# A decoder layer on one NeuronCore: two of four weight sums of the branch and gate products made in the SBUF ring by accumulating loads, and the products put in another order

## Chip, core and metric

The kernel runs on one core of one Trainium2 chip, from one launch. The metric is the time of the core for one execution in microseconds (us), as the median of several runs. Five engines with an instruction stream each work side by side: PE (TensorE, matrix products), ACT (ScalarE), DVE (VectorE), POOL (GpSimd) and SP (SyncE). Here SP issues the DMAs that load weights, and POOL issues those that copy and add in DRAM. Each engine executes its own stream in order; semaphores tie the streams together.

## What is computed

One layer: an input projection gives queries, keys and values for three token mixers and three gates; each mixer's output is projected (a branch), multiplied by the sigmoid of its gate and summed; then an output projection, LayerNorm, a squared-ReLU MLP and a gated input embedding. All in float32.

```python
proj = x @ w_in
(da_q, da_k, da_v, sb_q, sb_k, sb_v, dl_q, dl_k, dl_v, gates) = jnp.split(proj, ...)
g = jax.nn.sigmoid(gates).reshape(B, S, N_BRANCHES, D)
merged = (g[:, :, 0] * (o_da @ w_branch_da) + g[:, :, 1] * (o_sb @ w_branch_sb)
          + g[:, :, 2] * (o_dl @ w_branch_dil))
m = merged @ w_out
x = layer_norm(DEEPNORM_ALPHA * x + m, ln1_g, ln1_b)
c = jnp.square(jax.nn.relu(x @ w_up)) @ w_down
ple = jax.nn.sigmoid(x @ w_ple_gate) * (p @ w_ple)
x = layer_norm(DEEPNORM_ALPHA * x + c + ple, ln2_g, ln2_b)
```

S is 512, D is 1024. The branch weights of `w_branch_dil` (branch i=2) and `w_branch_da` (branch i=0) are 512x1024, `w_ple_gate` is 1024x1024.

## The kernel before

**Splits.** A float32 product is made of three fast ones: every operand is split into a high and a low part (`h`, `lo`), and PE computes h·h, h·lo and lo·h into one PSUM bank. For a weight chunk of 128x1024, `split_next` (L229) issues the cast of the raw chunk on ACT (L243, `wh<-raw`) and the subtract on DVE (L245, `wl<-raw,wh`). Raw chunks lie in a ring of RAW = 6 slots, which SP fills in order as slots come free (`fill`, L194, the load at L213); the split parts lie in rings of RING = 6.

**Seven products.** Large products are done with seven block products in place of eight (p = 1 to 7, Strassen's scheme in Winograd's form). The weight is cut into quarters w[0] to w[3]. Products 1, 2 and 4 use the quarters 0, 1 and 3 as they are; 5, 6, 7 and 3 use sums of two to four quarters. Those sums are made in DRAM on POOL's queue well ahead: `sum_steps` (L1083) yields one copy or one accumulating DMA (`accum_op` add) at a time, from `up_steps` (eight steps for all four sums) or `two_steps` (four steps for the sums of 5 and 6), and `issue` (L1116) ties each to the main stream. How fast they are yielded is set by a credit that each work item adds to: its size times its `rate` (default set at L825).

**Sums in the ring.** There is a second way, `chained` (L180), used by the value pair and by the gate products: the operand of product 7 is the one of product 1 plus a quarter, the operand of 3 that of 6 plus a quarter. `then_add` (L171) puts the quarter onto the raw slot by an accumulating DMA on POOL's queue as soon as the slot's first split is issued, and the slot is then split again:

```python
def add():
    nc.gpsimd.dma_start(s["raw"], src, accum_op=OP.add, max_dma_last_dim=4096)
c["then"] = add
return chunk_of(s)
```

**The places of the change.** `seven` (L603) with `gate_chain` (L668) makes the gate columns of one mixer: seven products in the order 1, 2, 7, 6, 4, 5, 3, two chunks to a product, two row halves r. Products 1, 6, 5 and 3 of a half share one PSUM bank ("x"), 7 and 4 another ("y"); `done` evacuates them into the tiles `graw`: by an ACT copy (L695), or a DVE add that also adds an earlier tile (L688 for product 4, L691 for product 5). Product 3 starts in bank x when product 5 of the same half has been evacuated from it.

`branch_seven` (L759) follows each gate chain: the branch of mixer i = 2, then of i = 0. It has one chunk to a product (K is 256 for a block), so its chunks follow each other twice as fast as those of a gate. Its forms of the mixer's output (`o7`, `o6`, `o4`, split at L271 and L272) come from `branch_forms` (L727). `pleg_items` (L991) is the gate of the input embedding: seven products of two chunks, beside LayerNorm 1, in which POOL computes the small tile `lr` (L872). Items follow each other in a list; the splits for the next items are issued ahead of their matmuls as ring slots allow, so that the first chunks of a branch are split while PE still works on the gate chain.

Of the kernel before, what the change touches and what calls it, by code (L numbers as in the profile page):

```python
# [10 lines left out]
F32 = mybir.dt.float32  # L11
# [7 lines left out]
P = 128  # L19
# [36 lines left out]
def trunk(tc, a, out):  # L56
    nc = tc.nc
    es = ExitStack()
    with es:
# [108 lines left out]
        def chunk(src, w):  # L168
            return chunk_of(load(src, w))
# [96 lines left out]
        def item(cs, mm, ev, need=None, bank=None, size=1.0):  # L266
            items.append({"c": cs, "mm": mm, "ev": ev, "need": need, "bank": bank, "size": size})
# [451 lines left out]
                         bank=at_bank if tt == 1 and not half else None)  # L719
                    items[-1]["rate"] = 2.4  # L720

        bsum = {i: [dram.tile([P, 1024], F32, name=f"bsum{i}_{j}") for j in range(4)] for i in (0, 2)}
        of = {}
        LATE = {0: 0, 2: 4}

        def branch_forms(i):

            o = [oT.pop(4 * i + k) for k in range(4)]
            f = {p: slot(f"o{p}") for p in (7, 6, 4)}

            def parts(p):
                return [f[p][:, c] for c in (HB, HC)]

            def whole(p):
                h, lo = split(f.pop(p), f"o{p}")
                of[p] = [(h[:, c], lo[:, c]) for c in (HB, HC)]

            for k in range(2):
                nc.vector.tensor_sub(parts(7)[k], o[2 + k][:, HC], o[k][:, HC])
            yield  # L740
            for p, q, k0 in ((6, 7, 0), (4, 6, 2)):
                for k in range(2):
                    nc.vector.scalar_tensor_tensor(parts(p)[k], parts(q)[k], -1.0, o[k0 + k][:, HB],
                                                   op0=OP.mult, op1=OP.subtract)
                yield
            sp = {k: split(o[k], "oT") for k in (2, 3)}
            yield
            for k in range(2):
                nc.vector.tensor_sub(o[k][:, HC], o[k][:, HB], o[k][:, HC])
                sp[k] = split(o[k], "oT")  # L750
            for p, k0, c in ((1, 0, HB), (5, 0, HC), (2, 2, HB), (3, 2, HC)):
                of[p] = [[t[:, c] for t in sp[k0 + k]] for k in range(2)]
            yield
            for p, n in ((7, LATE[i]), (6, LATE[i] // 4), (4, 0)):
                whole(p)
                for _ in range(n + 1):
                    yield

        def branch_seven(i, behind):  # L759

            s, b, cs = {}, {}, {}
            for p in (2, 1, 7, 6, 4, 5, 3):
                for r in range(2):
                    if not r:
                        blk = {1: 0, 2: 1, 4: 3}.get(p)
                        cs[p] = chunk(bsum[i][{5: 0, 6: 1, 7: 2, 3: 3}[p]] if blk is None else
                                      a["wbq"][i // 2, blk].rearrange("p k n -> p (k n)"), 1024)

                    def bank(p=p, r=r):
                        name = {1: "x", 6: "x", 5: "x", 3: "x", 7: "y", 4: "y", 2: "z"}[p]  # L770
                        if p in (1, 2, 7):
                            b[name, r] = at_bank()
                        return b[name, r]

                    def mm(ps, p=p, r=r):
                        q, c = slice(r * P, r * P + P), cs[p]
                        for k in range(2):
                            n = slice(k * 512, k * 512 + 512)
                            h, lo = of[p][k]
                            go, end = k == 0 and p in (1, 2, 7), k == 1 and p in (2, 3, 4)  # L780
                            nc.tensor.matmul(ps, h[:, q], c["h"][:, n], start=go, stop=False, skip_group_check=True)
                            nc.tensor.matmul(ps, h[:, q], c["l"][:, n], start=False, stop=False, skip_group_check=True)
                            nc.tensor.matmul(ps, lo[:, q], c["h"][:, n], start=False, stop=end, skip_group_check=True)

                    def ev(ps, p=p, r=r):
                        if p in (2, 7, 6):
                            s[p, r] = slot("b0")
                            nc.scalar.copy(s[p, r], ps)
                            return
                        v, to = {1: (2, (r, 0)), 4: (6, (r, 1)), 5: (7, (2 + r, 1)), 3: (None, (2 + r, 0))}[p]  # L790
                        if v is not None:
                            nc.vector.tensor_add(s[v, r], s[v, r], ps)
                        g = sg.pop((i, *to))
                        nc.vector.tensor_mul(g, g, ps if v is None else s[v, r])
                        m = merged[to]
                        (nc.vector.tensor_add if p in (1, 3) else nc.vector.tensor_sub)(m, m, g)
                    item([cs[p]] if r else [], mm, ev, need=[cs[p]], bank=bank, size=0.25)
                    items[-1]["rate"] = 1.0
                    to = {2: (r, 0), 7: (r, 1), 6: (2 + r, 1), 4: (2 + r, 0)}.get(p)
                    if to:  # L800
                        def pre(to=to):
                            sg[(i, *to)] = gate_sig(i, *to)
                        items[-1]["pre"] = pre
                    for t in behind.get((p, r), ()):
                        turn_item(*t)
# [16 lines left out]

        last_plain = len(items)
        for j, it in enumerate(items):
            it.setdefault("rate", 2.8 if j < 25 else 0.0 if j < 31 else 2.6)  # L825
        def first_gate(tt, half):
            g = gate_sig(1, tt, half)
            nc.vector.tensor_mul(merged[tt, half], merged[tt, half], g)
# [162 lines left out]
        def pleg_items():  # L991
# [5 lines left out]
            def gate(r, to, g, sign, z=None):  # L997
                tt, half = r + 2 * to[1], to[0]
                nc.scalar.activation(g, g if z is None else z, AF.Sigmoid, scale=sign)
                gated[tt, half] = g  # L1000
# [11 lines left out]
                    for _ in range(2):  # L1012
                        yield

            def operand(p, kp):
                blk = {1: 0, 2: 1, 4: 3}.get(p)
                src = a["wg"][kp, blk] if blk is not None else None
                return chunk(gsum[kp][{5: 0, 6: 1, 7: 2, 3: 3}[p]] if src is None else
                             src.rearrange("p k n -> p (k n)"), 1024)

            cs = {}
            for p in (2, 1, 7, 6, 4, 5, 3):
                for r in range(2):
                    name = {1: "x", 6: "x", 5: "x", 3: "x", 7: "y", 4: "y", 2: "z"}[p]
                    if not r:
                        cs[p] = [operand(p, kp) for kp in range(2)]

                    def bank(p=p, r=r, name=name):
                        if p in (1, 2, 7):
# [12 lines left out]
                            nc.tensor.matmul(ps, lo[:, q], c["h"][:, n], start=False, stop=end, skip_group_check=True)  # L1042

                    def ev(ps, p=p, r=r):
                        if p in (2, 7, 6):
                            s[p, r] = slot("sg2")
                            nc.scalar.copy(s[p, r], ps)
                        if p == 1:
                            nc.vector.tensor_add(s[2, r], s[2, r], ps)
                            gate(r, (0, 0), s[2, r], 1.0)  # L1050
# [1165 lines left out]
```

## Time and profile before

| | |
|---|---|
| median of three runs | 1036.57 us (1036.25 to 1037.67) |
| the profiled execution | 1035.76 us |
| its span, first to last instruction | 1033.6 us |
| mean granted clock of PE | 0.998 |
| ACT casts of weight chunks, L243 | 257, mean 1049 ns |
| DVE subtracts of weight chunks, L245 | 257, mean 1222 ns |
| DMA traffic | 249.19 MB, mean 241 GB/s |
| DMAs that POOL issues: share of 16 engines | 44.6% |
| DMAs that SP issues: share of 16 engines | 35.4% |

A row of the profile's tables by line has the line, the engine, the operation, and the tiles as out<-in, with buffer numbers left out. Rows in order of time begin with start and duration in us from the span's start; "x2" joins two of a kind that followed each other, and the bracket at the end gives the idle time of the engine before the row and what ended it. A DMA row on POOL is the issue alone; the time to landing is listed apart. Matmul rows overlap, since PE is pipelined: their starts tell the pace.

### The profile page before, as it was taken

What the parts mean: (1) busy time and instruction counts of PE and PEld (TensorE: products, weight loads), DVE (VectorE), ACT (ScalarE), POOL (GpSimd) and SP (SyncE); (2) the same over time, 40 slices, a digit from 0 to 9 for tenths busy, and PEclk for the clock granted to TensorE, in tenths of its full rate; (3) what the DMA queues carried; (4) which work ended last, traced back from release to release, by engine and by line L of the source; (5) the groups of instructions that cost most, each with busy time, mean ns of one, the idle gap of its engine ahead of it and who ended that gap; (6) DMA issues with size and microseconds to landing.
All of it is one profiled execution on the core that took longest, in us unless ns stands there. A gap on an engine that the chain in (4) does not pass through costs nothing.

```text
span 1033.6 us, 15019 instructions
## 1 busy us (share of the span) xinstructions
PE 1025.3 (99%) x5434; PEld 880.5 (85%) x5434; DVE 782.9 (76%) x1412; ACT 593.0 (57%) x1012; POOL 180.6 (17%) x271
## 2 busy tenths in 40 slices
PE   9999999999999999999999999999999999999997
PEld 7888888889888888888888888889999899899886
DVE  7888667758764657779788895798768777777966
ACT  7565544535434646576575743776666556566651
POOL 0002411121211232411011030111111111111001
PEclk9999999999999999999999999999999999999999
DMA  8349969495976999977889895479999999999512
GB/s 310 122 159 272 287 184 226 107 295 146 282 187 212 272 276 289 252 203 202 249 250 223 269 320 201 142 215 339 333 311 336 301 303 331 306 298 308 185 61 81
DMA packets 71321, 249.19 MB, mean 241 GB/s; under 512 B 8808, under 2 KB 9592, under 8 KB 71248
## 3 DMA queue, kind: packets, MB, share of 16 engines
q0 software_dynamic: 32464, 116.21, 44.6%
q1 hardware_dynamic: 38208, 131.13, 35.4%
q8 instruction: 42, 0.69, 0.3%
q10 hardware_dynamic: 576, 0.92, 0.2%
q14 instruction: 31, 0.25, 0.1%
HBM read 246.10 MB, written 98.59 MB: 333 GB/s over the span
## 4 chain that ended last, share of the span: by engine, by line
PE 97%; DVE 2%; ACT 0%; issue 0%; DVEq 0%
PE mm L87 10%; PE mm L89 10%; PE mm L88 10%; PE at L1300 4%; PE at L1301 4%; PE at L1302 4%; PE at L618 3%; PE at L620 3%; PE at L619 3%; PE mm L495 2%; PE mm L497 2%; PE mm L496 2%; PE at L89 1%; PE at L88 1%; PE at L87 1%; PE at L910 1%
## 5 line engine op out<-in xcount | busy, mean ns | idle before, releaser
L243 ACT CAST wh<-raw 128x1024 fp32r<-128x1024 f32 x257 | 268.5, 1049 | 237.0 <-PE mm L88 127.1
L245 DVE TENSOR_TENSOR wl<-raw,wh 128x1024 fp32r<-128x1024 f32 x257 | 312.2, 1222 | 118.9 <-ACT wh L243 117.6
L87 PE MATMUL mm<-xhT,wh 128*128 128x512 f32 x302 | 119.2, 395 | 0.0
L89 PE MATMUL mm<-xhT,wl 128*128 128x512 f32 x302 | 118.3, 392 | 0.0
L88 PE MATMUL mm<-xlT,wh 128*128 128x512 f32 x302 | 118.2, 392 | 0.0
L1300 PE MATMUL at<-wh,hh 128*128 128x512 f32 x188 | 73.7, 392 | 0.0
L1301 PE MATMUL at<-wl,hh 128*128 128x512 f32 x188 | 73.7, 392 | 0.0
L1302 PE MATMUL at<-wh,hl 128*128 128x512 f32 x188 | 73.1, 389 | 0.0
L87 PE MATMUL mm<-x1hT,wh 128*128 128x256 f32 x256 | 72.8, 285 | 0.0
L88 PE MATMUL mm<-x1lT,wh 128*128 128x256 f32 x256 | 72.4, 283 | 0.0
L89 PE MATMUL mm<-x1hT,wl 128*128 128x256 f32 x256 | 72.4, 283 | 0.0
L89 PEld LDWEIGHTS mm<-xhT,wl 128*128 128x128 f32 x302 | 56.7, 188 | 12.0
L87 PEld LDWEIGHTS mm<-xhT,wh 128*128 128x128 f32 x302 | 56.7, 188 | 11.3 <-PE mm L497 0.2
L88 PEld LDWEIGHTS mm<-xlT,wh 128*128 128x128 f32 x302 | 56.8, 188 | 10.8
L87 PEld LDWEIGHTS mm<-x1hT,wh 128*128 128x128 f32 x256 | 48.9, 191 | 1.9
L88 PEld LDWEIGHTS mm<-x1lT,wh 128*128 128x128 f32 x256 | 48.9, 191 | 1.5
L89 PEld LDWEIGHTS mm<-x1hT,wl 128*128 128x128 f32 x256 | 48.9, 191 | 0.0
L1118 POOL DMA_DIRECT2D usum<-in_wu_dram x32 | 28.3, 904 | 105.5 <-DVE wl L245 42.2
L1118 POOL DMA_DIRECT2D dsum<-in_wd_dram x28 | 25.2, 922 | 99.5 <-DVE wl L245 58.4
L1302 PEld LDWEIGHTS at<-wh,hl 128*128 128x128 f32 x188 | 35.3, 188 | 7.7
L1300 PEld LDWEIGHTS at<-wh,hh 128*128 128x128 f32 x188 | 35.5, 189 | 6.1
L1301 PEld LDWEIGHTS at<-wl,hh 128*128 128x128 f32 x188 | 35.5, 189 | 5.7
(628 smaller groups left out, 2670.2 us busy)
## 6 DMA issues: line engine op xcount, KB each, us to landing
usum<-in_wu_dram POOLq DMA_DIRECT2D x48, 512.0 KB, 9.2
dsum<-in_wd_dram POOLq DMA_DIRECT2D x42, 512.0 KB, 8.8
raw<-in_wt_dram SPq DMA_DIRECT2D x38, 512.0 KB, 5.7
raw<-usum SPq DMA_DIRECT2D x32, 512.0 KB, 7.6
raw<-dsum SPq DMA_DIRECT2D x28, 512.0 KB, 7.8
raw<-in_wd_dram SPq DMA_DIRECT2D x25, 512.0 KB, 6.4
raw<-in_wu_dram SPq DMA_DIRECT2D x24, 512.0 KB, 7.3
raw<-in_wv_dram SPq DMA_DIRECT2D x18, 512.0 KB, 5.3
```

Source lines behind the costliest of these rows:

```text
L87: nc.tensor.matmul(ps, wh, xh, start=start, stop=False, skip_group_check=True)
L88: nc.tensor.matmul(ps, wh, xl, start=False, stop=False, skip_group_check=True)
L89: nc.tensor.matmul(ps, wl, xh, start=False, stop=stop, skip_group_check=True)
L243: i = nc.scalar.copy(h, raw)
L245: i = nc.vector.tensor_sub(lo, raw, h.bitcast(F32))
L618: nc.tensor.matmul(ps, h[:, q], c["h"][:, n], start=go, stop=False, skip_group_check=True)
L619: nc.tensor.matmul(ps, h[:, q], c["l"][:, n], start=False, stop=False, skip_group_check=True)
L620: nc.tensor.matmul(ps, lo[:, q], c["h"][:, n], start=False, stop=end, skip_group_check=True)
L1118: i = nc.gpsimd.dma_start(o, i, accum_op=OP.add, max_dma_last_dim=4096)
L1300: nc.tensor.matmul(ps, h[:, q], c["h"][:, s], start=go, stop=False, skip_group_check=True)
L1301: nc.tensor.matmul(ps, h[:, q], c["l"][:, s], start=False, stop=False, skip_group_check=True)
L1302: nc.tensor.matmul(ps, lo[:, q], c["h"][:, s], start=False, stop=end, skip_group_check=True)
```

## The change

The dilated branch (i = 2) and the differential branch (i = 0) take their operands by `chained`, and so does the gate of the input embedding. `bsum` and `gsum` go from four tiles to two and are made by `two_steps`. Products 1 and 2 change places in both, and 6 and 7 in the branches, with the evacuations, the forms and the gate signals that belong to them. The default rate of items from number 49 on is 2.1 in place of 2.6.

```diff
-        bsum = {i: [dram.tile([P, 1024], F32, name=f"bsum{i}_{j}") for j in range(4)] for i in (0, 2)}
+        bsum = {i: [dram.tile([P, 1024], F32, name=f"bsum{i}_{j}") for j in range(2)] for i in (0, 2)}
...
-            for p, n in ((7, LATE[i]), (6, LATE[i] // 4), (4, 0)):
+            for p, n in ((6, LATE[i]), (7, LATE[i] // 4), (4, 0)):
...
         def branch_seven(i, behind):
 
             s, b, cs = {}, {}, {}
-            for p in (2, 1, 7, 6, 4, 5, 3):
+            w = [a["wbq"][i // 2, n].rearrange("p k n -> p (k n)") for n in range(4)]
+            for p in (1, 2, 6, 7, 4, 5, 3):
                 for r in range(2):
                     if not r:
-                        blk = {1: 0, 2: 1, 4: 3}.get(p)
-                        cs[p] = chunk(bsum[i][{5: 0, 6: 1, 7: 2, 3: 3}[p]] if blk is None else
-                                      a["wbq"][i // 2, blk].rearrange("p k n -> p (k n)"), 1024)
+                        cs[p] = [chained(cs, p, 0, w, bsum[i])]
...
-                        if p in (2, 7, 6):
+                        if p in (1, 7, 6):
                             s[p, r] = slot("b0")
                             nc.scalar.copy(s[p, r], ps)
                             return
-                        v, to = {1: (2, (r, 0)), 4: (6, (r, 1)), 5: (7, (2 + r, 1)), 3: (None, (2 + r, 0))}[p]
+                        v, to = {2: (1, (r, 0)), 4: (6, (r, 1)), 5: (7, (2 + r, 1)), 3: (None, (2 + r, 0))}[p]
...
-                    to = {2: (r, 0), 7: (r, 1), 6: (2 + r, 1), 4: (2 + r, 0)}.get(p)
+                    to = {1: (r, 0), 6: (r, 1), 7: (2 + r, 1), 4: (2 + r, 0)}.get(p)
...
-            it.setdefault("rate", 2.8 if j < 25 else 0.0 if j < 31 else 2.6)
+            it.setdefault("rate", 2.8 if j < 25 else 0.0 if j < 31 else 2.6 if j < 49 else 2.1)
...
-            def operand(p, kp):
-                blk = {1: 0, 2: 1, 4: 3}.get(p)
-                src = a["wg"][kp, blk] if blk is not None else None
-                return chunk(gsum[kp][{5: 0, 6: 1, 7: 2, 3: 3}[p]] if src is None else
-                             src.rearrange("p k n -> p (k n)"), 1024)
+            def operand(cs, p, kp):
+                return chained(cs, p, kp, [a["wg"][kp, i].rearrange("p k n -> p (k n)") for i in range(4)], gsum[kp])
...
-            for p in (2, 1, 7, 6, 4, 5, 3):
+            for p in (1, 2, 7, 6, 4, 5, 3):
...
-        gsum = [[dram.tile([P, 1024], F32, name=f"gsum{m}_{i}") for i in range(4)] for m in range(2)]
+        gsum = [[dram.tile([P, 1024], F32, name=f"gsum{m}_{i}") for i in range(2)] for m in range(2)]
...
-                    todo.append(up_steps(bsum[2 * (n == 1)], a["wbq"][int(n == 1)]))
-            todo.extend(up_steps(gsum[m], a["wg"][m]) for m in range(2))
+                    todo.append(two_steps(bsum[2 * (n == 1)], a["wbq"][int(n == 1)]))
+            todo.extend(two_steps(gsum[m], a["wg"][m]) for m in range(2))
```

In the instruction streams SP has 268 rows before and 260 after, POOL 275 and 267; ACT and DVE keep their counts, 912 and 1384. Three places show what moves. The first is ACT's stream at the start of branch i = 2, between the gate chain's work (graw); the chunks are the raw tiles, oTh, o7h and o6h are high parts of the mixer's output. Before:

```order
L243 CAST wh_5196<-raw_5141 128x1024
L565 ACTIVATE graw_5151<-graw_5151 128x512
L271 CAST oTh_5210<-oT_3119 128x512
L243 CAST wh_5243<-raw_5143 128x1024
L271 CAST o7h_5227<-o_1113_5096 128x512
L243 CAST wh_5249<-raw_5145 128x1024
L565 ACTIVATE graw_5067<-graw_5067 128x512
L695 COPY graw_5268<-at_4969 128x512
```

and now, with one row more ahead to show the first chunk:

```order
L243 CAST wh_5175<-raw_5120 128x1024
L271 CAST oTh_5187<-oT_2837 128x512
L243 CAST wh_5180<-raw_5126 128x1024
L565 ACTIVATE graw_5136<-graw_5136 128x512
L271 CAST oTh_5192<-oT_3111 128x512
L243 CAST wh_5225<-raw_5128 128x1024
L271 CAST o6h_5209<-o_1114_5082 128x512
L243 CAST wh_5230<-raw_5120 128x1024
L565 ACTIVATE graw_5052<-graw_5052 128x512
L695 COPY graw_5251<-at_4954 128x512
```

The order of kinds is the same; the last cast of a chunk (product 6 before, 7 now) reads the slot of product 1, raw_5120, a second time, where before it read one of its own.

The second is DVE's stream at the same place, now:

```order
L245 TENSOR_TENSOR wl_5176<-raw_5120,wh_5175 128x1024
L245 TENSOR_TENSOR wl_5181<-raw_5126,wh_5180 128x1024
L272 TENSOR_TENSOR oTl_5188<-oT_2837,oTh_5187 128x512
L691 TENSOR_TENSOR graw_5052<-graw_5052,at_4954 128x512
L272 TENSOR_TENSOR oTl_5193<-oT_3111,oTh_5192 128x512
L245 TENSOR_TENSOR wl_5226<-raw_5128,wh_5225 128x1024
L272 TENSOR_TENSOR o6l_5210<-o_1114_5082,o6h_5209 128x512
L245 TENSOR_TENSOR wl_5231<-raw_5120,wh_5230 128x1024
L691 TENSOR_TENSOR graw_5077<-graw_5077,at_4971 128x512
```

Before, the same kinds stand in the same order, with raw_5145 in the last subtract; behind it in both stands the gate chain's evacuation of product 5, half 1 (L691).

The third is POOL's stream there, now:

```order
L176 DMA raw_4806<-in_wgm_dram 128x1024
L176 DMA raw_4808<-in_wgm_dram 128x1024
L1114 DMA dsum_3_135<-in_wd_dram 128x1024
L1116 DMA dsum_0_136<-in_wd_dram 128x1024
L176 DMA raw_5120<-in_wbq_dram 128x1024
L176 DMA raw_5128<-in_wbq_dram 128x1024
L1116 DMA usum_0_112<-in_wu_dram 128x1024
```

The two adds from in_wbq are new: raw_5120 becomes the operand of product 7, raw_5128 that of product 3. Before, the DMAs between the gate chains' adds (in_wgm) were sum steps for the MLP alone.

More of the change, by code (lines that the diff above doesn't have):

```diff
@@ L775, in mm @@
                     def mm(ps, p=p, r=r):
-                        q, c = slice(r * P, r * P + P), cs[p]
+                        q, c = slice(r * P, r * P + P), cs[p][0]
                         for k in range(2):
@@ L795, in ev @@
                         m = merged[to]
-                        (nc.vector.tensor_add if p in (1, 3) else nc.vector.tensor_sub)(m, m, g)
-                    item([cs[p]] if r else [], mm, ev, need=[cs[p]], bank=bank, size=0.25)
+                        (nc.vector.tensor_add if p in (2, 3) else nc.vector.tensor_sub)(m, m, g)
+                    item(cs[p] if r else [], mm, ev, need=cs[p], bank=bank, size=0.25)
                     items[-1]["rate"] = 1.0
-                    to = {2: (r, 0), 7: (r, 1), 6: (2 + r, 1), 4: (2 + r, 0)}.get(p)
+                    to = {1: (r, 0), 6: (r, 1), 7: (2 + r, 1), 4: (2 + r, 0)}.get(p)
                     if to:
@@ L1025, in pleg_items @@
                     if not r:
-                        cs[p] = [operand(p, kp) for kp in range(2)]
+                        cs[p] = [operand(cs, p, kp) for kp in range(2)]
                     def bank(p=p, r=r, name=name):
@@ L1044, in ev @@
                     def ev(ps, p=p, r=r):
-                        if p in (2, 7, 6):
+                        if p in (1, 7, 6):
                             s[p, r] = slot("sg2")
                             nc.scalar.copy(s[p, r], ps)
-                        if p == 1:
-                            nc.vector.tensor_add(s[2, r], s[2, r], ps)
-                            gate(r, (0, 0), s[2, r], 1.0)
+                        if p == 2:
+                            nc.vector.tensor_add(s[1, r], s[1, r], ps)
+                            gate(r, (0, 0), s[1, r], 1.0)
                         elif p == 4:
```

## The prediction

> **What bounds it now.** I read the profile's first page, then the table of waits of TensorE (PE), then tables by stretches of the span, and last the rows around the places where the edit moves work. From the page, parts 1 and 4 (busy us, share, count; then the chain that ended last):
>
> ```profile
> PE 1025.3 (99%) x5434; PEld 880.5 (85%) x5434; DVE 782.9 (76%) x1412; ACT 593.0 (57%) x1012; POOL 180.6 (17%) x271
> ```
>
> ```profile
> PE 97%; DVE 2%; ACT 0%; issue 0%; DVEq 0%
> ```
>
> The table of PE's waits has a single row (line, releaser: total us, times, longest), and the table by stretches shows busy us and counts, the granted clock, the DMA share and GB/s:
>
> ```profile
> PE at L1495 <- DVE zero L1492: 1.2, 1, 1.2
> ```
>
> ```profile
> 400.00:450.00 50.00, 49.79 (x261) 41.82 (x260) 37.55 (x112) 30.96 (x76) 18.96 (x26) 1.00 1.03 270
> 500.00:525.00 25.00, 25.00 (x112) 20.71 (x111) 19.54 (x27) 16.67 (x23) 3.06 (x4) 1.00 0.82 236
> 525.00:550.00 25.00, 25.00 (x112) 20.54 (x111) 20.80 (x27) 17.65 (x25) 4.75 (x6) 1.00 0.90 239
> ```
>
> PE is the bound: 97% of the chain, and no engine but DVE at the very start holds it for a listed time. The matmuls come evenly, as five PE rows show (start, duration, engine, line, operation):
>
> ```profile
> 528.96 0.39 PE L781 MATMUL at<-wh,oTh 128*128 128x512 f32 x1
> 529.18 0.39 PE L782 MATMUL at<-wl,oTh 128*128 128x512 f32 x1
> 529.41 0.39 PE L783 MATMUL at<-wh,oTl 128*128 128x512 f32 x1
> 529.63 0.39 PE L781 MATMUL at<-wh,oTh 128*128 128x512 f32 x1
> 529.86 0.46 PE L618 MATMUL at<-wh,xhT 128*128 128x512 f32 x1
> ```
>
> One starts every 0.22 to 0.23 us; the two 25-us stretches hold 112 each at DMA shares of 0.82 and 0.90, so the traffic doesn't slow the stream. In 400 to 450 us, where the DMA share is 1.03, PE lacks 0.21 us of 50. Saved DMA work can buy next to nothing; whatever makes PE wait costs its whole length, since nothing behind PE can give it back.
>
> **The change, part by part.**
>
> *What it removes.* The page's list of DMA issues (count, KB each, median us to landing):
>
> ```profile
> bsum<-in_wbq_dram POOLq DMA_DIRECT2D x12, 512.0 KB, 7.8
> raw<-bsum SPq DMA_DIRECT2D x8, 512.0 KB, 5.5
> ```
>
> With the branch operand of products 7 and 3 made in the ring, bsum loses half of its sums and loads (the ple gate's gsum the same): 16 sum steps fewer and 8 adds into the ring more on POOL's queue, 8 loads fewer on SP's. No PE row waits for these loads, so I cost it at nothing. The cover is the even PE stream above; without it the gain would be what PE lacks, 0.21 us in the one stretch where it lacks anything. The lower default rate (2.1) spaces the remaining sums for the MLP; fewer are left to make, and no load of them is on PE's list of waits: 0.
>
> *What it adds: a landing between two splits.* In branch_seven the first chunk is now the quarter for product 1. After its split (ACT cast L243, DVE subtract L245) POOL issues the accumulating DMA of `then_add` (L176), and the fourth chunk, product 7, is that slot again: its cast waits for the landing. Before, the fourth chunk was a load that SP had brought long ago. ACT and DVE run in order, so what stands behind that cast and its subtract waits too. Rows for branch i=2, ACT then DVE (x2 is two instructions in one row):
>
> ```profile
> 519.68 1.05 ACT L243 CAST wh<-raw 128x1024 fp32r<-128x1024 f32 x1
> ...
> 526.60 1.05 ACT L243 CAST wh<-raw 128x1024 fp32r<-128x1024 f32 x1
> ```
>
> ```profile
> 521.60 2.36 DVE L245 TENSOR_TENSOR wl<-raw,wh 128x1024 fp32r<-128x1024 f32 x2
> ...
> 526.20 1.22 DVE L245 TENSOR_TENSOR wl<-raw,wh 128x1024 fp32r<-128x1024 f32 x1 [0.45 <-ACT wh L243]
> 527.35 0.68 DVE L272 TENSOR_TENSOR o7l<-o,o7h 128x512 fp32r<-128x512 f32 x1
> 527.95 1.22 DVE L245 TENSOR_TENSOR wl<-raw,wh 128x1024 fp32r<-128x1024 f32 x1
> 529.09 0.68 DVE L691 TENSOR_TENSOR graw<-graw,at 128x512 f32<-128x512 f32 x1
> ```
>
> The last row is the gate chain's evacuation of product 5. It ends at 529.09 + 0.68 = 529.77, and the PE row at 529.86 (L618, first matmul of gate product 3, which fills the same PSUM bank) starts 0.09 later. So between the fourth cast at 526.60 and this matmul there is hardly slack: the chain is cast, subtract, evacuation, matmul, 529.86 − 526.60 = 3.26 us, of which 0.27 is DVE busy with `o7l` (the cast ends at 527.65, the subtract starts at 527.95; at 526.17 to 526.20 the same hand-over took 0.03). With a late cast that 0.27 falls away: 2.99.
>
> How late is the cast? The first subtract ends at 521.60 + 1.22 = 522.82. POOL starts an add 0.29 after its release, by the second of these rows; the other three are the places that the next steps use:
>
> ```profile
> 503.31 0.84 POOL L176 DMA_DIRECT2D raw<-in_wgm_dram  x1 [0.29 <-DVE wl L245]
> 503.85 0.85 POOL L1120 DMA_DIRECT2D dsum<-in_wd_dram  x1
> 516.84 0.83 POOL L1118 DMA_DIRECT2D usum<-in_wu_dram  x1 [12.14 <-DVE wl L245]
> ```
>
> That makes 523.11. I have to set the latency from there to landing. The trace has 16 adds of the same kind and size (value pair and gate chains, L176), with who waited for them:
>
> ```profile
>   ACT wh L243: 5.3, 2
> ...
> DMA to landing us min/median/max: 5.3/6.6/10.5
> ```
>
> and two single ones, their starts on POOL (idle before in brackets) and then their us to landing in the same order:
>
> ```profile
> 484.04 0.85 POOL L176 DMA_DIRECT2D raw<-in_wgm_dram  x1 [18.23 <-DVE wl L245]
> ...
> 540.93 0.87 POOL L176 DMA_DIRECT2D raw<-in_wgm_dram  x1 [1.90 <-DVE wl L245]
> ```
>
> ```profile
> raw<-in_wgm_dram POOLq DMA_DIRECT2D x1, 512.0 KB, 5.5
> ...
> raw<-in_wgm_dram POOLq DMA_DIRECT2D x1, 512.0 KB, 8.4
> ```
>
> An idle queue gave 5.5, one that had issued a DMA 1.9 us before gave 8.4. ACT has waited for an add twice already; those casts had cover behind them, this one has not. With 0.08 from landing to cast, my allowance, PE's matmul starts at 523.11 + latency + 0.08 + 2.99 = 526.18 + latency, against 529.86: **stall = latency − 3.68**. Bounds: 1.6 us at 5.3 and 6.8 at 10.5. POOL's previous DMA stands some 6 us earlier (the row at 516.84), so the queue is nearly empty: between 5.5 and the median 6.6 I take 6.0, giving 2.3.
>
> Branch i=0 is built alike. Its rows, DVE, ACT, PE:
>
> ```profile
> 578.89 2.35 DVE L245 TENSOR_TENSOR wl<-raw,wh 128x1024 fp32r<-128x1024 f32 x2
> ...
> 585.24 1.22 DVE L245 TENSOR_TENSOR wl<-raw,wh 128x1024 fp32r<-128x1024 f32 x1
> 586.38 0.68 DVE L691 TENSOR_TENSOR graw<-graw,at 128x512 f32<-128x512 f32 x1
> ```
>
> ```profile
> 583.89 1.04 ACT L243 CAST wh<-raw 128x1024 fp32r<-128x1024 f32 x1
> ```
>
> ```profile
> 587.15 0.46 PE L618 MATMUL at<-wh,xhT 128*128 128x512 f32 x1
> ```
>
> Subtract ended 580.11 or 580.12, add from 580.40, cast to matmul 587.15 − 583.89 = 3.26, less the 0.28 between 584.93 + 0.03 and 585.24, so 2.98. Stall = 580.40 + latency + 0.08 + 2.98 − 587.15 = latency − 3.69; with 6.0 again 2.3 (1.6 to 6.8).
>
> The Trainium skill, "DMA: Bandwidth & Descriptors", section "Anatomy of one DMA — SWDGE (gpsimd) path", gives a fit for one such DMA: about 2.0 us fixed plus bytes over 436 GB/s. For 512 KB that is an estimate of 3.2 us, and by it both stalls would be below zero and the sum 0. The trace disagrees, since the shortest of 16 adds took 5.3.
>
> *The other add of the branch.* Product 6's slot is accumulated for product 3. Its split ends at 526.20 + 1.22 = 527.42, so the add starts near 527.7; product 3's chunk, the seventh, is cast here:
>
> ```profile
> 534.78 1.05 ACT L243 CAST wh<-raw 128x1024 fp32r<-128x1024 f32 x1
> ```
>
> That is 7.1 us of cover, 9.4 with the stall of 2.3 ahead of it. Only an add of over 9.4 would be late; I take 0. A slot that is used twice also comes free later for SP's next load, but that load is for a chunk six casts on: 0.
>
> *The ple gate.* It has two chunks to a product. ACT and DVE rows of its first chunk and of product 7's first:
>
> ```profile
> 653.23 1.06 ACT L243 CAST wh<-raw 128x1024 fp32r<-128x1024 f32 x1
> ...
> 665.72 1.10 ACT L243 CAST wh<-raw 128x1024 fp32r<-128x1024 f32 x1
> ```
>
> ```profile
> 654.32 1.22 DVE L245 TENSOR_TENSOR wl<-raw,wh 128x1024 fp32r<-128x1024 f32 x1 [1.06 <-ACT wh L243]
> ```
>
> Subtract to 655.54, add from 655.83, needed at 665.72: 9.9 us of cover, against 6.6 typical. POOL also makes LayerNorm's small `lr` there, and each add queues ahead of the next `lr` for its issue, 0.84 us by the row at 503.31; an `lr` is made from DVE work that runs after that same subtract, so I cost it at 0 (bound: 0.8).
>
> *The swaps* of products 1 and 2, and of 6 and 7, keep the number and size of every PE, ACT and DVE instruction: 0.
>
> *Sum.* The profiled execution took 1035.76 us, 2.2 more than its span of 1033.6; 1035.76 + 2.3 + 2.3 = 1040.4. The median of the three runs, 1036.57, is 0.8 above the profiled one, so for timed runs I say **1041.2**.
>
> **The rivals.**
>
> *Slow adds.* An add that shares the queues takes 8.4 like the second single row: 8.4 − 3.7 at each site, together 9.4 in place of 4.6, time 1046.0. For it: the DMA share is 0.9 there. Against: POOL's previous DMA is 6 us old there, where the 8.4 followed another after 1.9 us idle.
>
> *The cover holds (the other side: not slower).* The place is the fourth cast of each branch, the price is latency − 3.7, and it decides at an add landing within 3.7 us: then PE's matmul at 529.86 starts as before, and the time is 1036.6. The skill's formula says this. Against it stand all 16 rows. It would also come true if the matmul at 529.86 did not in fact depend on the evacuation, but 0.09 us behind it, lengthened to 0.46 where others take 0.39, speaks for dependence.
>
> *Freed traffic shows.* 24 operations fewer and 8 more leave the queues emptier; PE gains its missing 0.21 us and perhaps a little at the start. 1036.3, no measurable change; for over 0.2% another mechanism would be needed, and PE at 99% leaves only the ends of the span.
>
> *Late MLP sums.* The rate of 2.1 delays a sum until its load is late, at one place, by one step: a sum step takes 7.8 by the bsum row; a slip of one would add up to that, 1044 without and 1049 with the branch stalls. Against: no load of a sum is on PE's list of waits now, and 16 steps fewer stand ahead.
>
> **How the numbers follow.** Forecast 0.68, slow adds 0.12, cover holds 0.10, freed traffic 0.06, late sums 0.04. About 0.2% (2.1 us) is what a measurement of this kernel tells from no change. Of the forecast some 0.02 falls below that, since two latencies of 4.7 would be needed. Slower: 0.66 + 0.12 + 0.04 = 0.82; same: 0.02 + 0.10 + 0.03 = 0.15; faster: the other 0.03 of freed traffic. The likeliest case alone spans 1039.8 (5.3 at both sites, +3.2) to 1044 (about 7.4 at both). The range, 1037.5 to 1046.5, takes in the slow adds above; below it stops short of no change, leaving out 0.16 at that end and a few hundredths at the other.
>
> **What would show it.** After the change, PE's table of waits should have a new row, L618 released by DVE `graw` (L691), of about 2.3 us twice; ACT's casts should wait for `raw<-in_wbq` adds, and these should land 5.3 to 8.4 us after issue. The span before 520 us and after 590 us should be as long as now. I am wrong if the adds land within 3.7 us, if PE waits at the ple gate or for a sum in the MLP, or if the time grew without a PE wait at these two places.

## The result

The changed kernel took 1042.31 us as the median of 6 runs (1041.84 to 1043.73), the one before 1036.53 (6 runs, 1036.25 to 1037.67): 5.8 us slower, ratio 1.0056 with an interval of 1.0045 to 1.0067. The profiled execution took 1043.73 us, the slowest of the six, with a span of 1041.7 against 1033.6 before.

TensorE's waits in the changed kernel (line, releaser: total us, times, longest):

```profile
PE at L618 <- DVE graw L691: 4.5, 2, 2.5
PE at L1491 <- DVE zero L1488: 1.2, 1, 1.2
PE at L347 <- ACT wh L243: 0.2, 1, 0.2
```

The first row is new and is the one that was forecast, twice, and in sum 4.5 where 4.6 was said. The page, part 1, shows something that was not:

```profile
PE 1028.6 (99%) x5434; PEld 883.2 (85%) x5434; DVE 783.9 (75%) x1412; ACT 592.8 (57%) x1012; POOL 175.6 (17%) x263
```

TensorE executes the same 5434 instructions, yet is busy for 1028.6 us where it was 1025.3. So 4.5 of waits, 3.3 of longer work and the 0.2 at L347 make 8.0 of the 8.1 by which the span grew. Where the 3.3 us lie shows the table by stretches of the span around the first wait (busy us of PE, PEld, DVE, ACT, POOL; then granted clock, the share of its full speed that TensorE gets, DMA share, GB/s):

```profile
530.00:532.00 2.00, 0.09 (x1) 0.00 (x0) 1.82 (x2) 1.76 (x4) 0.00 (x0) 1.00 0.92 178
532.00:533.00 1.00, 0.96 (x4) 0.83 (x5) 0.00 (x0) 0.63 (x1) 0.00 (x0) 1.00 0.98 270
533.00:534.00 1.00, 1.00 (x4) 0.76 (x4) 0.00 (x0) 0.00 (x0) 0.00 (x0) 0.60 1.02 414
534.00:535.00 1.00, 1.00 (x4) 0.81 (x3) 0.00 (x0) 0.95 (x1) 0.00 (x0) 0.50 1.00 410
535.00:536.00 1.00, 1.00 (x4) 0.72 (x3) 0.87 (x1) 0.10 (x1) 0.00 (x0) 0.50 0.15 57
536.00:537.00 1.00, 1.00 (x5) 0.82 (x4) 0.35 (x1) 0.39 (x1) 0.35 (x1) 0.70 0.00 0
537.00:538.00 1.00, 1.00 (x6) 0.83 (x5) 0.31 (x1) 1.00 (x2) 0.20 (x1) 1.00 0.55 156
```

TensorE stands still for 1.95 us, starts again at full clock, and a microsecond later the granted clock goes to 0.5 until about 536.5. The shortfalls of the clock column, 0.4 + 0.5 + 0.5 + 0.3, are 1.7 us of work lost behind this wait. Behind the second, which ends at 593.64, it is the same:

```profile
594.00:595.00 1.00, 1.00 (x5) 0.85 (x4) 0.79 (x2) 0.82 (x2) 0.00 (x0) 0.82 0.97 176
595.00:596.00 1.00, 1.00 (x4) 0.71 (x4) 0.00 (x0) 0.22 (x1) 0.00 (x0) 0.50 1.09 201
596.00:598.00 2.00, 2.00 (x6) 1.62 (x5) 1.14 (x1) 0.83 (x1) 0.00 (x0) 0.50 0.93 287
```

Twice 1.7 makes the 3.3 to within 0.1. The rows of PE show it too: the pitch, from start to start, goes from 0.23 to 0.43.

```profile
529.70 0.39 PE L780 MATMUL at<-wh,oTh 128*128 128x512 f32 x1
532.04 0.50 PE L618 MATMUL at<-wh,xhT 128*128 128x512 f32 x1 [1.95 <-DVE graw L691]
532.38 0.39 PE L619 MATMUL at<-wl,xhT 128*128 128x512 f32 x1
...
534.24 0.63 PE L619 MATMUL at<-wl,xhT 128*128 128x512 f32 x1
534.66 0.63 PE L620 MATMUL at<-wh,xlT 128*128 128x512 f32 x1
535.09 0.63 PE L618 MATMUL at<-wh,xhT 128*128 128x512 f32 x1
```

And the chain behind the first wait, ACT's cast of the fourth chunk, then DVE, and the adds' us from issue to landing (the first at 523.18, the second at 584.18 on POOL):

```profile
529.08 1.05 ACT L243 CAST wh<-raw 128x1024 fp32r<-128x1024 f32 x1 [2.32 <-DMA raw<-in_wbq_dram]
```

```profile
530.16 1.22 DVE L245 TENSOR_TENSOR wl<-raw,wh 128x1024 fp32r<-128x1024 f32 x1 [2.06 <-ACT wh L243]
531.30 0.68 DVE L691 TENSOR_TENSOR graw<-graw,at 128x512 f32<-128x512 f32 x1
```

```profile
raw<-in_wbq_dram POOLq DMA_DIRECT2D x1, 512.0 KB, 5.8
...
raw<-in_wbq_dram POOLq DMA_DIRECT2D x1, 512.0 KB, 6.4
```

The cast stands at 529.08 where it stood at 526.60, for no reason but the landing; the evacuation is queued behind it, and the gate's product 3 behind that.

### The profile page after: what moved, and what is told of

Same layout as the page of the kernel before. It is cut to its first block, busy times and chain, and to the rows that moved or that the text cites. A ratio compares the mean times of both kernels' runs of the same rounds, so it can differ in the third digit from the quotient of the medians.

```text
span 1041.7 us, 14996 instructions
## 1 busy us (share of the span) xinstructions
PE 1028.6 (99%) x5434; PEld 883.2 (85%) x5434; DVE 783.9 (75%) x1412; ACT 592.8 (57%) x1012; POOL 175.6 (17%) x263
## 4 chain that ended last, share of the span: by engine, by line
PE 86%; issue 5%; DVE 3%; DMA 3%; ACT 2%; POOL 1%; DVEq 0%; SPq 0%; POOLq 0%; ACTq 0%
PE mm L87 10%; PE mm L89 10%; PE mm L88 10%; PE at L1296 4%; PE at L1297 4%; PE at L1298 4%; PE mm L495 2%; PE mm L497 2%; PE mm L496 2%; PE at L88 1%; PE at L89 1%; PE at L87 1%; PE at L908 1%; PE at L910 1%; PE at L909 1%
```

## The experiments

The theory: the adds to product 7's operand land too late, TensorE waits, and each wait is followed by a stretch at half clock. Twelve experiments were run: ten further kernels, and the changed kernel and one of the ten a second time. The diffs show the lines that matter, with cuts marked by "...". The ratios are against the kernel before on the same chip.

### Which part of the change: the branches as before

`branch_seven`, `branch_forms` and `bsum` are those of the kernel before; the ple gate and the rate stay changed.

```diff
...
-                    todo.append(two_steps(bsum[2 * (n == 1)], a["wbq"][int(n == 1)]))
+                    todo.append(up_steps(bsum[2 * (n == 1)], a["wbq"][int(n == 1)]))
```

> The changed kernel with the two branches as before (operands of products 7 and 3 from four sums in DRAM, old order of products); the ple gate's adds in the ring and the rate of 2.1 stay. Theory (all of the loss comes from the adds of the branches): no wait of TensorE at L618, a granted clock of 1.00 from 525 to 600 us, 1036.5 us like before, within 0.8. Rival (the part of the loss that is no wait, 3.3 us of busy time of TensorE, comes from the ple gate, the rate or the lighter sums): about 1039 to 1040, with the busy time of TensorE near 1028.

Measured 1036.11 us (10 runs), ratio 0.9998 (0.9988 to 1.0007); no wait at L618, TensorE busy for 1025.2 us. All of the loss comes from the branches, its 3.3 us of longer work too.

### Which add: only product 3's operand in the ring

```diff
-                        cs[p] = [chained(cs, p, 0, w, bsum[i])]
+                        cs[p] = [chunk(bsum[i][2], 1024) if p == 7 else chained(cs, p, 0, w, bsum[i])]
...
```

(`bsum` has three tiles then, made in six steps.)

> The changed kernel, but the operand of product 7 of the branches is a sum in DRAM again; only that of product 3 is made in the ring. Theory (the distance from product 1 to product 7, three chunks, is too short, that from 6 to 3 is enough): no wait, 1036.5 within 0.8. Rival (any add inside a branch with one chunk to a product lands late): a wait of over 0.5 us behind the seventh cast near 535 us, and 1038 to 1041.

Measured 1035.51 us (10 runs), ratio 0.9992 (0.9982 to 1.0001), the only wait of over half a microsecond being that at the start. The add from product 6 to product 3 is covered; the one from 1 to 7 does the harm.

### How the wait follows the landing: a shorter add

The add for product 7 covers only the first columns, so the rest of the quarter is missing from that operand; the waits in the program are the same.

```diff
+            cols, times = (64, 1) if src.tensor.name.startswith("in_wbq") and s.get("seven") else (1024, 1)
...
-                nc.gpsimd.dma_start(s["raw"], src, accum_op=OP.add, max_dma_last_dim=4096)
+                for _ in range(times):
+                    nc.gpsimd.dma_start(s["raw"][:, :cols], src[:, :cols], accum_op=OP.add, max_dma_last_dim=4096)
...
```

> The changed kernel, but the add that makes product 7's operand in the two branches covers 64 of the 1024 columns; the rest of the quarter is left out of that operand. Everything waits as before, only the landing comes sooner. Theory (the wait is the latency of the add less 3.7 us, and the clock follows the wait): a latency of 2.5 to 3.7, no wait at L618, clock 1.00, 1036.0 to 1036.8. Rival (the wait comes from the semaphore chain or the queue, not from the time of the transfer): latency above 5, waits as in the changed kernel, 1041 to 1043.

Measured 1035.54 us (10 runs), ratio 0.9994 (0.9985 to 1.0003), latencies of 2.7 and 3.0, no wait at L618. (The profiles of this kernel and the next have a wait of 1.1 us in the MLP, too, which no other has.)

> The same with 512 of the 1024 columns; the other half of the quarter is left out. Theory: a latency of 4 to 5, a wait of 0.3 to 1.3 us at each of the two places, and if the fall of the clock needs a gap of some length, a clock of 1.00 behind them: 1037 to 1039. Rival (any gap of TensorE, however short, makes the clock fall for 3.4 us): 1.7 us more at each place, 1040.5 to 1042.5.

Measured 1037.02 us (10 runs), ratio 1.0010 (0.9998 to 1.0022). In the profile the latencies are 3.9 and 4.2, and the wait is

```profile
PE at L621 <- DVE graw L694: 0.4, 1, 0.4
```

(L621 and L694 are L618 and L691 of the changed kernel) with a clock of 1.00 behind it. One of the ten runs took 1042.75 at a mean clock of 0.995; it has no trace.

> The changed kernel with the add for product 7 over 768 of the 1024 columns, the rest left out of that operand. Latency 4.7 to 5.3 by the 3.9 to 4.2 for 512 columns and the 5.8 to 6.4 for all, so waits of 1.0 to 1.6 us at each place. Theory (a gap of up to 1.8 us left the clock alone, of 1.95 and more did not): clock 1.00 behind both, 1037.8 to 1039.4. Rival (a gap of any length above half a microsecond is followed by half clock): 1041 to 1043.

Measured 1040.78 us (4 runs: 1038.30, 1039.89, 1041.67, 1042.71), ratio 1.0042 (1.0027 to 1.0056). The profile is of the run of 1039.89: latencies of 5.0 and 4.9, and

```profile
PE at L621 <- DVE graw L694: 3.1, 3, 1.7
```

with a clock of 1.00 from 528 to 540 and from 588 to 598 us. That profile agrees with the theory, but the median does not: the two slower runs had a mean clock of 0.997 and 0.996, the two faster 0.998. So some of these executions seem to have had half clock too; whether their waits were longer is not known, since no trace of a slower one was kept.

Latency of the add against TensorE's wait, all from profiles, beside "latency less 3.7":

| add | latency, us | wait forecast | wait measured |
|---|---|---|---|
| 64 columns | 2.7, 3.0 | 0, 0 | none |
| 512 columns | 3.9, 4.2 | 0.2, 0.5 | none listed, 0.4 |
| 768 columns | 5.0, 4.9 | 1.3, 1.2 | 1.2, 1.7 (and one of 0.3) |
| all 1024 | 5.8, 6.4 | 2.1, 2.7 | 1.95, 2.54 |
| all, second profile | 6.2, 6.0 | 2.5, 2.3 | 2.38, 2.15 |

The rule holds to 0.2 us but for one wait that was 0.5 longer. (The forecast is the delay of the matmul. A listed wait is 0.16 shorter, since it begins at the end of the matmul before, 0.39 after that one's start, and the next start was due 0.23 after it.) At the place of the exception the add was issued at 583.28, only 6.1 us before the matmul's turn at 589.40; in the changed kernel it is issued 6.75 before it, at 523.18 for 529.93 and at 584.18 for 590.93. So "less 3.7" holds only while VectorE makes the first split as early as there.

### The clock: fill the wait with work

Fourteen extra matmuls go into product 3, half 0, of each gate chain, ahead of the matmul that waits.

```diff
+                            if k == 3 and (p, r) == (3, 0) and "fill" in bank_of:
+                                for _ in range(14):
+                                    nc.tensor.matmul(ps, h[:, q], c["h"][:, n], start=False, stop=False, skip_group_check=True)
...
```

> The changed kernel with 14 extra matmuls in product 3, half 0, of each gate chain (128x512, all into its own sum, so these gate columns come out with other values), which TensorE does while the add lands: 14 times 0.227 is 3.2 us at each of the two places. The four branch matmuls that stood ahead of the wait now stand behind it, so 3.2 fills the wait of 1.95 + 0.91 or 2.54 + 0.91 almost wholly. Theory (the granted clock falls to half for about 3.4 us because TensorE stood still for 2 us): no fall of the clock near 530 and 590 us, time 1036.5 + 2 x 3.2 + 0.3 = 1043.2. Rival (the clock falls for a reason that the stillness has nothing to do with, the traffic of the adds or the burst of work behind them): it falls here too, TensorE is busy 3.3 us longer, and the time is 1046 to 1047.

Measured 1043.03 us (4 runs, 1042.00 to 1046.57), ratio 1.0068 (1.0049 to 1.0086); the three other runs had a mean clock of 0.998, the profiled one, the slowest, 0.996. Its profile holds both outcomes. At the first place the add took 6.1 us, the fourteen matmuls covered it, and no stretch is throttled. At the second the add took 8.7, and a wait was left over:

```profile
PE at L621 <- DVE graw L694: 2.5, 1, 2.5
```

```profile
525.00:533.00 8.00, 7.99 (x36) 6.31 (x35) 4.62 (x6) 3.65 (x5) 1.39 (x2) 1.00 0.93 195
533.00:545.00 12.00, 12.00 (x55) 9.91 (x54) 8.07 (x10) 9.68 (x15) 1.63 (x3) 1.00 0.80 280
...
596.00:598.00 2.00, 2.00 (x8) 1.57 (x7) 0.89 (x2) 2.00 (x5) 0.00 (x0) 0.70 0.91 254
598.00:600.00 2.00, 2.00 (x7) 1.52 (x6) 1.23 (x1) 0.72 (x1) 0.00 (x0) 0.50 0.11 45
600.00:602.00 2.00, 2.00 (x10) 1.67 (x9) 0.69 (x1) 1.77 (x3) 0.55 (x1) 0.95 0.37 119
```

With the same late add and no standstill the clock stays at 1.00; with a standstill of 2.54 us it falls. The rival, that the traffic or the work behind the add lowers it, is out for these places; two kernels below (the evacuation first, the longer add) have late adds too, no standstill of 1.95 us or more there, and a clock of 1.00.

### The same once more

> The changed kernel itself once more, for a second profile of it. Theory (each wait is a latency less 3.7, and each gap of about 2 us or more is followed by one stretch at half clock): span less 1033.6 equals the waits plus 1.7 per stretch, to 0.4 us. Rival (the timed runs, 1.5 us faster than the profiled one, have shorter waits but the same clock loss, or no clock loss at one of the places): the split between the two terms differs from the first profile; it tells which.

Measured 1043.22 us (4 runs, 1042.26 to 1044.79), ratio 1.0064 (1.0047 to 1.0081); the profile is of a run of 1044.10 with a span of 1042.1:

```profile
PE at L618 <- DVE graw L691: 4.5, 2, 2.4
```

```profile
PE 1029.2 (99%) x5434; PEld 883.7 (85%) x5434; DVE 783.8 (75%) x1412; ACT 592.4 (57%) x1012; POOL 176.3 (17%) x263
```

```profile
530.25 0.39 PE L780 MATMUL at<-wh,oTh 128*128 128x512 f32 x1
533.02 0.80 PE L618 MATMUL at<-wh,xhT 128*128 128x512 f32 x1 [2.38 <-DVE graw L691]
```

Waits of 4.5 and 3.9 us of longer work make 8.4 of the 8.5 by which this span is over 1033.6. Waits plus 1.7 for each stretch would make 7.9, so the theory misses by 0.6, more than the 0.4 that it allowed. But 0.55 of that was lost ahead of the first wait: the matmul before it starts at 530.25 here and at 529.70 in the first profile. Against the 529.63 of the kernel before, 0.62 and 0.07 us were lost up to there, which leaves 7.9 of the 8.5 here and 8.0 of the 8.1 in the first profile: behind that point both lose the same. The first matmul behind the wait already runs slowly here (0.80 us): the half clock began about 0.2 us before the standstill ended. Two of the four runs took 1042.3 and one 1044.79, all at a mean clock of 0.996; whether the faster ones lost less clock or had shorter waits can't be read from runs without a trace.

### The order on VectorE: the evacuation first

The kernel has a set of items behind whose matmuls no split is issued; here product 5 of the gate chains is put into a second such set, so that `graw` (L691, L693 here) stands ahead of the late subtract.

```diff
-            pump(freed, 0 if n < 10 or ple_at - 1 <= n <= ple_at + 1 or n in sums_first else 2)
+            pump(freed, 0 if n < 10 or ple_at - 1 <= n <= ple_at + 1 or n in sums_first or n in evac_first else 2)
...
```

> The changed kernel, but around product 5 of the gate chains no split is issued behind the matmuls, so that on VectorE the evacuation of product 5, half 1, stands ahead of the subtract of the branch's fourth chunk; the add, its landing and the late cast stay. Theory (the add hurts only because the evacuation queues behind the late subtract): no wait at L618, no fall of the clock, 1036.5 within 0.8. Rival (the late operand itself, or ScalarE's late copies behind the cast, holds TensorE a few matmuls later): a wait of 1 to 2.5 us moves to L780 to L783 or to another line of the gate, and the time is 1039 to 1042.

Measured 1038.51 us (10 runs), ratio 1.0019 (1.0010 to 1.0029). The theory fell in part. The wait at L618 is gone, and the clock stays at 1.00 through both gate chains and branches, but two waits stand later:

```profile
PE mm L815 <- DVE b L797: 1.8, 1, 1.8
...
PE at L782 <- DVE b L793: 0.6, 1, 0.6
```

L793 and L797 are the branch's own evacuations, L815 the transposes of the merged sum: the branch now waits for its own work. Whether the late landing delays that work, or the edit itself, which holds back splits, was not told apart.

```profile
600.47 0.44 PE L815 MATMUL mm<-ident,b 128*128 128x128 f32 x2 [1.81 <-DVE b L797]
```

This wait of 1.81 us was not followed by half clock.

### A longer add

The add for product 7 is made twice in a row, so the quarter counts twice in that operand.

> The changed kernel with that add made twice, one behind the other, so the quarter is counted twice in product 7's operand. Latency twice 5.5 to 6.5, waits of 7.5 to 9.5 us at each place. Theory (the clock is at half for one stretch of about 3.4 us behind a gap, however long): 1.7 us on top of each wait, busy time of TensorE near 1028.6 as in the changed kernel, 1054.5 to 1059. Rival (the loss grows with the gap, as 1.7 per 2.2 us would): 6 to 7 us more at each place, busy time near 1038, 1063 to 1069.

Measured 1045.05 us (2 runs), ratio 1.0082 (1.0062 to 1.0103). It doesn't answer the question it was made for: the program's scheduler put the evacuation ahead of the late subtract by itself, as in the kernel above (L694 at 528.20, the subtract at 536.37), so the long wait at L618 did not arise. Instead

```profile
PE at L783 <- ACT b L790: 4.8, 5, 1.7
```

and three of under a microsecond: 6.5 us of waits in eight pieces, none over 1.7, with a mean clock of 0.999. Many short stops, and no half clock. TensorE was also busy 2.4 us longer than before. By estimate the restarts account for 2.2 of it: at the longest stop two starts are 2.11 us apart (537.14 and 539.25) for a listed wait of 1.72 and a usual pitch of 0.23, and the next start follows after 0.33, which is 0.27 more than the listed wait, eight times.

### The mend: product 7 one chunk later

```diff
-            for p in (1, 2, 6, 7, 4, 5, 3):
+            for p in (1, 2, 6, 5, 7, 4, 3):
...
```

Product 5 is copied and product 7 added onto it, where it was the other way round; gate signals follow, and two transposes that need product 4's part move behind product 3.

> The changed kernel with the branch's products in the order 1, 2, 6, 5, 7, 4, 3: product 5 changes places with 7, so the chunk made from product 1's slot is the fifth and not the fourth; both adds stay in the ring (the evacuations of 5 and 7, their gate signals and two transposes follow). The fifth cast of the kernel before stood at 531.51 against 526.60 for the fourth, so an add started at 523.1 has 8.4 us of cover in place of 3.5. Theory (only the distance was wrong): latencies of 5.8 to 6.4 are covered, no wait at L618, clock 1.00, 1035.5 to 1036.2 like the kernel with one add to a branch. Rival (the operand of product 7 comes too late for the products behind it, as when the evacuation was put first): a wait of 1 to 2 us at L780 to L782 or at the transposes, 1037.5 to 1039.

Measured 1037.92 us (11 runs), ratio 1.0014 (1.0005 to 1.0022): the rival's time, with smaller waits at the transposes than it had, and not the theory's 1036.2 or less. But there is no wait at L618, with latencies of 6.0 and 6.4; the fifth cast, at the first place, waits for TensorE, not for the add:

```profile
531.75 1.05 ACT L243 CAST wh<-raw 128x1024 fp32r<-128x1024 f32 x1 [0.58 <-PE at L620]
```

Of the 1.65 us that are left, 0.8 show as waits around the moved transposes:

```profile
616.02 0.88 PE L813 MATMUL mm<-ident,b 128*128 128x128 f32 x6 [0.43 <-DVE b L795]
617.24 0.50 PE L908 MATMUL at<-wh,mh 128*128 128x512 f32 x1 [0.35 <-ACT mh L817]
```

To tell the order from the transposes, the new order was then used in the dilated branch alone; the differential branch got product 7's sum from DRAM and kept its transposes:

> The changed kernel with the order 1, 2, 6, 5, 7, 4, 3 in the dilated branch alone, both of its adds in the ring; the differential branch keeps its order and gets product 7's sum from DRAM, so no transpose is moved. Theory (with the distance of four chunks an add to product 7 costs nothing, and the 1.65 us of the kernel with both branches so came from the moved transposes): no wait of TensorE beyond the first, 1035.5 to 1036.5. Rival (the late product 7 costs something in the branch itself): 1036.9 to 1037.5 with a wait or a stretched pitch between 540 and 555 us.

Measured 1035.91 us (11 runs) against 1036.73, ratio 0.9992 (0.9983 to 1.0001); no wait of TensorE but 1.2 at the start and 0.3 at L347, and an add of 6.0 us that nothing waits for. Four chunks of distance are enough for latencies of 6.0 to 6.4, and the 1.65 us arise in the differential branch; how much of them is its transposes and how much its order was not told apart.

### Is any of them faster than before?

The kernel with only product 3's operand in the ring was run once more.

> The kernel with product 7's sum in DRAM and product 3's operand in the ring once more, to see whether it is faster than the one before: 1035.5 against 1036.4 in the first job, with an interval that touched no change. Theory (fewer DMAs and no new wait are worth some 0.8 us): ratio 0.9992 with an interval below 1. Rival (the first job's difference was chance): ratio 0.9997 to 1.0003.

Measured 1036.07 us (11 runs) against 1036.27, ratio 1.0000 (0.9991 to 1.0009): the 0.9 us of its first measurement did not come again. None of the kernels without the waits is shown to be faster than the one before.

## Why the prediction was right, and by how much it was short

**The bound, and what removal is worth.** TensorE's stream set the end, and fewer DMAs bought nothing that can be measured: ratio 0.9998 with the branches restored, and 0.9992 to 1.0000 in the kernels that keep part of the adds and have no wait. Shown.

**The place and the mechanism of the loss.** Both waits stand where they were forecast, with the releaser that was named, and the rule "latency less 3.7" held over latencies from 2.7 to 6.4, with the one exception above. The steps of the chain came as forecast: the add was issued 0.29 after the subtract, the cast started 0.1 after the landing, and the matmul 2.96 after the cast where 2.99 was said. I had taken 6.0 for both adds; they took 5.8 and 6.4. The sum of waits, 4.6, came out as 4.5. The estimate of 3.2 us by the fit of the Trainium skill ("DMA: Bandwidth & Descriptors", section "Anatomy of one DMA — SWDGE (gpsimd) path") was too low for these adds into the ring: 5.8 and 6.4 in the first profile, and 2.7 even for 32 KB.

**The step that was short.** "Whatever makes PE wait costs its whole length" was taken as the whole cost. It is the lower bound: in both profiled executions each of the two waits also cost 1.7 us at half clock, a term that the sum put at nothing. So the sum, 4.6, is to be set against 8.0 in the profiled execution and 5.8 in the median of runs. Both times lie inside the span of the likeliest case, 1039.8 to 1044, but that span had been opened for latencies up to 7.4, not for a slower clock; that 1041.2 came within 1.1 us of the median is partly luck. Why the timed runs lost less than the profiled ones stays open; the last section has a likely reason. The kernel before held the hint, in the last microseconds of its own table by stretches, where TensorE has stopped:

```profile
1026.00:1028.00 2.00, 0.81 (x7) 0.60 (x6) 1.15 (x4) 0.00 (x0) 0.36 (x3) 1.00 0.55 208
1028.00:1030.00 2.00, 0.00 (x0) 0.00 (x0) 2.00 (x5) 0.00 (x0) 0.52 (x1) 0.95 0.00 0
1030.00:1032.00 2.00, 0.00 (x0) 0.00 (x0) 0.56 (x2) 0.00 (x0) 0.00 (x0) 0.50 0.69 243
```

Its last matmuls end near 1026.8, and within some 3 us the clock is at half.

**The order behind the late cast.** That the evacuation is queued behind the late subtract was right, but it is not the only thing that the late chunk holds up: with the evacuation first, 2.0 us stayed, as waits in the branch itself, though the edit that put it first may have a part in them.

**What was costed at nothing.** The add from product 6 to 3 (cover 7.1 us) and the ple gate's adds are covered: in the changed kernel the first of the latter was issued at 663.89 and took 5.6, and product 7's first chunk was cast at 673.77. The swaps of products and the lower rate are in the restored kernel or in the kernel with one add, and cost nothing there.

## What to carry to other kernels

When an operand is made by a DMA that is issued in the stream, count the work between its issue and its use in microseconds of the bounding engine, and set that against the slowest of such DMAs in the trace; three chunks were 2 us too few here, four were enough. Where TensorE is the bound, price a new wait of 2 us or more at its length, and up to 1.7 us on top, since half clock may follow it. An instruction that waits for a landing holds up what is queued behind it, so look first for evacuations there; yet putting them ahead gains only until the late operand itself is due.

## What the runs showed of the hardware

Standstills of TensorE of 1.95, 2.54, 2.38, 2.15 and 2.54 us, in three profiles, were each followed by a stretch of some 3.4 us at a granted clock of 0.5, which began about a microsecond behind the standstill in three of them and about 0.2 us from its end in two, once before it and once after. Standstills of 1.81, 1.7 and 1.2 us in other profiles were not followed by one. The Trainium skill, "TensorE: Matmul & The Clock Gate", section "Part 1: The HAM clock gate (the "warmup" mystery)", has the clock follow the activity in windows of about 3.4 us that run free of the program; the length of the stretches and their shifting start agree.

The traces show such windows. In the first profile of the changed kernel the clock falls at 533.20 (the 0.60 of the microsecond from 533), at 594.64 (the 0.82 from 594), and at 1038.38, where the kernel has no more matmuls. The distances, 61.44 and 443.74 us, are 18 and 130 times 3.413. In the second profile (532.80, 594.24, 1037.98) both distances are the same, and in the kernel with the fourteen matmuls the one from 596.78 to 1040.52 is 443.74 too, though the windows lie elsewhere in the program each time. With windows of that length, laid back from the fall of the clock at the end of each profile, TensorE's idle time within a window tells what follows:

| kernel | window, us | TensorE idle in it, us | clock in the next window |
|---|---|---|---|
| changed | 529.78 to 533.20 | 1.95 | 0.50 |
| changed | 591.22 to 594.64 | 2.42 | 0.50 |
| changed, second profile | 529.38 to 532.80 | 2.16 | 0.50 |
| changed, second profile | 590.82 to 594.24 | 2.15 | 0.50 |
| fourteen matmuls | 593.37 to 596.78 | 2.27 | 0.50 |
| branches as before, its end | 1025.45 to 1028.86 | 2.11 | 0.50 |
| 512 columns, its end | 1027.77 to 1031.19 | 1.87 | 1.00 |
| evacuation first | 598.00 to 601.42 | 1.81 | 1.00 |

In all fourteen profiles, every window with 1.95 us or more of idle time was followed by half clock for one window at least, and none with 1.87 or less behind the start of the kernel. So in these runs the limit lies between 1.87 and 1.95 of 3.41 us. A wait of 2.0 to 2.5 us that falls across the bound of two windows can leave less than that in each and cost its own length alone. That would explain why the timed runs lost less than the profiled ones; no trace of such an execution was kept, so this is not shown. The advice to avoid idle gaps of over 3.4 us (the Trainium skill, "TensorE: Matmul & The Clock Gate", section "HAM oscillation — how this bites in real kernels") is too mild for what is seen here, where 2 us were enough.
